# A mixer recorded as tasks with element-exact dependencies and issued from a list schedule

## The chip, the cores and the metric

The kernel runs on one core of one Trainium2 chip. The metric is the device time of one execution in microseconds. TensorE (PE) multiplies matrices, PEld is its weight load, VectorE (DVE), ScalarE (ACT) and GpSimd (POOL) work on tiles in the on-chip memories SBUF and PSUM, and SyncE (SP) mostly issues DMA transfers. Each engine runs its own instructions in the order in which the program lists them and waits on semaphores for the others. So the order on each engine is a part of the program.

## The reference

A decoder trunk of two layers over 16 learned tokens and 1024 input tokens, model width 1024, everything in float32. Layer 0 mixes tokens by RWKV-7 (8 heads of 64) beside a pooling mixer, layer 1 by differential attention; an MLP stands behind each. The part that the change touches is layer 0's mixer:

```python
y = h @ w_in                                   # 1024 -> 14 tiles shifted, 4 pooled
ys = ys + (prev - ys) * mu                     # shift by one token
def step(S, inp):                              # the recurrence, over tokens
    r_t, w_t, k_t, v_t, kk_t, a_t = inp
    sa = jnp.einsum('bhvk,bhk->bhv', S, -kk_t)
    S = (S * w_t[:, :, None, :] + sa[..., None] * (kk_t * a_t)[:, :, None, :]
         + v_t[..., None] * k_t[:, :, None, :])
    o = jnp.einsum('bhvk,bhk->bhv', S, r_t)
    return S, o
o = group_norm(o) * ln_w + ln_b + bonus        # then times a gate g
z = pooled differences of u (windows 2, 4, 8, 16) @ pool_w
return jnp.concatenate([o, z], axis=-1) @ w_out
```

## The kernel before

Activations lie with channels on the 128 partitions and tokens along the free dimension, in blocks of 346 or 348 tokens for the projections and 260 (`NH`) for the output projection. A float32 product is made of three matmuls in a faster format (`mm3`, lines 213 to 219): high part of the weights times high part of the input, low times high, high times low.

Layer 0's mixer is `mixer0` (line 1331). After the entry and `lora` (low-rank paths; their tiles are `psl`, `psg`, `lg`), about 82 us into the run, it works on four things that depend on one another loosely:

- `project` (line 976): one of 18 tiles of the input projection into PSUM tile `ps`, shifted and written to DRAM (`yd`).
- `prep` (line 1094) for each of four head pairs: products within chunks of 64 tokens (tiles `w`, `zb`, `pss`, `sa`, `sb`, `sg`), packed and written to DRAM as `pk`. `invert` (line 1190): 31 small VectorE steps (`tm`, `xi`) that invert the chunks' triangular blocks, read back as `ds`.
- `chain` (line 1216) for each head pair: 17 chunks in groups of up to two, nine groups. Each group loads `lt`, makes block-diagonal tiles `bd` on POOL, three rounds of matmuls into `xs` with copies `x1` (ScalarE) and differences `x2` (VectorE) between them, then `gb`, `qp`, `mk`, `qq`, and for each chunk the output `ob` and the next state: two matmuls accumulate into `sp` (lines 1267 and 1269), and ScalarE writes `S` from it. Every four chunks the output is normed (tiles `ft`, matmul line 1283) and written to DRAM as `ozd`.
- `early` (line 359): parts of the output projection whose inputs exist (PSUM tile `pse`, 18 matmuls each, copied to `pz` by ScalarE and sent to DRAM as `part`), and `pool_group` (line 1292).

What sets the order is a table, `PLAN` (line 60), of stages; `braid` (line 283) takes one step after another from the generators of a stage, at the rates in the table. The instructions are then placed by the framework's scheduler, with program order as their priority. The last two stages read

```python
(('early', 8, 4), ('invert', 3, 3), ('chain', 2, 1)), (('early', 24, 1), ('chain', 3, 2))
```

Behind the mixer stands `late` (line 402): the rest of the output projection, norms and the MLP. It is built otherwise: each piece of work is a task in a `Flow` (line 76), with an engine, a cost by formula and names that it reads and writes; `order` (line 112) ranks each task by the longest path behind it and fills a list schedule; `run` (line 160) issues the tasks in this order, which the framework then keeps. `late_weight` (line 394) loads two of its weights, `wl`, ahead of the last stage through SP's queue; ScalarE rounds each into a high part (`opb`) and VectorE takes the rest.

Of the kernel before, what the change touches and what calls it, by code (L numbers as in the profile page):

```python
# [7 lines left out]
F32 = mybir.dt.float32  # L8
# [67 lines left out]
class Flow:  # L76
# [6 lines left out]
    def add(self, eng, cost, fn, r, w, port=False, size=0, tail=0.0):  # L83
# [8 lines left out]
        i = len(self.tasks)  # L92
        self.tasks.append((eng, cost, fn, deps, port, size, tail))
        for x in r:
            self.read.setdefault(x, set()).add(i)
        for x in w:
            self.wrote[x] = i
            self.read[x] = set()

# [65 lines left out]

class Trunk:
# [18 lines left out]
    def nm(self, s):  # L185
        self.uid += 1
        return f"{s}{self.uid}"

# [24 lines left out]
    def mm3(self, ps, ws, xs, first=True, last=True):  # L213
        nc = self.nc
        n = len(ws)
        for i, ((wh, wl), (xh, xl)) in enumerate(zip(ws, xs)):
            nc.tensor.matmul(ps, wh, xh, start=(first and i == 0), stop=False)  # L217
            nc.tensor.matmul(ps, wl, xh, start=False, stop=False)  # L218
            nc.tensor.matmul(ps, wh, xl, start=False, stop=(last and i == n - 1))  # L219
# [174 lines left out]
    def late_weight(self, l, i, ne):  # L394
        nc = self.nc
        raw = self.R[0][:, i % 2, :self.lw_n[i]]
        hi, lo = self.lw(i)
        nc.sync.dma_start(raw, self.lw_src(l, i))
        nc.scalar.copy(hi, raw)
        nc.vector.tensor_tensor(lo, raw, hi.bitcast(F32), op=ALU.subtract)  # L400

    def late(self, l, xs, part, hin, hmid, hout, pre, rsb):
# [107 lines left out]
        for i in range(len(n)):  # L510
            hi, lo = self.lw(i)
            if l or i > 1:
                z = ("R", i % 4 // 2, i % 2)
                raw = R[i % 4 // 2][:, i % 2, :n[i]]
                F.dma(lambda raw=raw, i=i: nc.sync.dma_start(raw, self.lw_src(l, i)), n[i] * 512, w=[z])
# [506 lines left out]
    def yload(self, mt, a, b):  # L1022
        y = self.yp.tile([P, 320], F32, tag="yl", name=self.nm("yl"), bufs=5)
        self.ylq.dma_start(y[:, :b - a], self.yd[mt, :, a + 1:b + 1])
        return y
# [91 lines left out]
    def prep_group(self, p, g0, m, e, ys, la, bo):  # L1117
# [45 lines left out]
        sb = self.mps.tile([P, 2, 4, C], F32, tag="p", name=self.nm("sb"))  # L1163
        for i in range(m):
            nc.tensor.matmul(sa[:, i, 2:4], kbd[:, i], w4[:, i, 1:3], start=True, stop=True)
        for i in range(m):
            nc.tensor.matmul(sa[:, i, 0:2], bbd[:, i], w4[:, i, 1:3], start=True, stop=True)
        for i in range(m):
# [3 lines left out]
        nc.vector.tensor_tensor(sg[:, :m, 0:4:2], sa[:, :m, 0:4:2],  # L1172
                                cb[:, None, None, B_MA:B_MA + C].broadcast_to([P, m, 2, C]), op=ALU.mult)
        nc.scalar.copy(sg[:, :m, 1:4:2], sa[:, :m, 1:4:2])
# [41 lines left out]
    def chain(self, p):  # L1216
# [5 lines left out]
        for f0, f1 in ((0, 1), (1, 5), (5, 9), (9, 13), (13, 17)):  # L1222
            ob = self.ops_.tile([P, 2, 4 * C], F32, tag="o", name=self.nm("ob"))
            for g0 in range(f0, f1, 2):
# [33 lines left out]
                for i in range(n):  # L1258
# [3 lines left out]
                    if gi:  # L1262
                        nc.tensor.matmul(ob[:, 0, io], S, qq[:, i, 1], start=True, stop=False)
                    nc.tensor.matmul(ob[:, 0, io], vb, qq[:, i, 0], start=gi == 0, stop=True)
                    if gi + 1 < NCH:
                        sp = self.fps.tile([P, P], F32, tag="s", name=self.nm("sp"))
                        nc.tensor.matmul(sp, mk[:, i, 0], vb, start=True, stop=gi == 0)
                        if gi:
                            nc.tensor.matmul(sp, mk[:, i, 1], S, start=False, stop=True)
                        S = cp.tile([P, P], F32, tag="S", name=self.nm("S"), bufs=3)  # L1270
# [8 lines left out]
            bon, gg, sq, x, rs = [ft() for _ in range(5)]  # L1279
# [5 lines left out]
            d = x  # L1285
# [6 lines left out]
    def pool_group(self, gi):  # L1292
# [3 lines left out]
        for t0, W in self.ch:  # L1296
            n = 16 + W
            u = tile()
            nc.sync.dma_start(u[:, :n], self.yd[14 + gi, :, PAD + 1 + t0 - 16:PAD + 1 + t0 + W])
            s = u  # L1300
            step = 1
            while step < win:
                x = tile()
# [4 lines left out]
            if t0 == 0:  # L1308
                ic = cb[:, B_IC + 16 * gi:B_IC + 16 * gi + 16]
                x = tile()  # L1310
# [20 lines left out]
    def mixer0(self):  # L1331
# [10 lines left out]
        with tc.tile_pool(name="yp", bufs=4) as self.yp:  # L1342
# [9 lines left out]
            with tc.tile_pool(name="dps", bufs=4, space=PSUM) as self.dps, \  # L1352
                 tc.tile_pool(name="mps", bufs=4, space=PSUM) as self.mps:
                with tc.tile_pool(name="lyp", bufs=1) as lyp:
# [10 lines left out]
                    self.lora(ly)  # L1365
            self.nw = 2
# [10 lines left out]
            with tc.tile_pool(name="dps", bufs=2, space=PSUM, reuse_waits="tile") as self.dps, \  # L1377
# [5 lines left out]
                 tc.tile_pool(name="cp", bufs=5, reuse_waits="tile") as self.cp:  # L1383
# [10 lines left out]
                with tc.tile_pool(name="pp", bufs=6, reuse_waits="tile") as self.pp:  # L1394
                    self.rwkv_tiles()
                    for _ in proj(*(4, 0, 8)[1:]):
                        pass
                    xs = [[] for _ in self.quarters]
                    rest = self.early(xs, A["wo_0"], part, 6, 6)
                    make = {"prep": self.prep, "invert": self.invert, "chain": self.chain, "proj": lambda a: proj(*a), "pool": lambda a: pools(*a),  # L1400
                            "load": lambda a: self.loads(xs, self.ozd, a, 0, 4), "early": lambda n: itertools.islice(rest, n)}
                    stage = lambda items: self.braid([(make[kind](arg), rate) for kind, arg, rate in items])
                    for items in PLAN[:-1]:
                        stage(items)
                self.base = contextlib.ExitStack()
                pool = self.base.enter_context(tc.tile_pool(name="base", bufs=1, side="right", reuse_waits="tile"))
                self.R = [pool.tile([P, 2, 1024], F32, name="raw0")]
                self.WP = [pool.tile([P, 2, 512], F32R, name=self.nm("wp")) for _ in range(3)]
                self.rsp = contextlib.ExitStack()
                self.rsa = self.rsp.enter_context(tc.tile_pool(name="rsp", bufs=1, side="right", reuse_waits="tile")).tile([P, T], F32, name="rsa")  # L1410
                self.ahead(0)
# [456 lines left out]
```

## Time and profile before

| | us |
|---|---|
| median of three runs | 2830.45 (2830.03 to 2833.7) |
| the profiled execution | 2842.85 |
| its span, first to last instruction | 2841.0 |
| mixer, from the first recorded work to the last chain's norm | 82 to 688, 606 |
| seam from there to the late part's dense start | 688 to 706 |

The profile comes from one execution, which took 12.4 us more than the median. In its rows "out<-in" names the tiles written and read, without their numbers; "x" is a count; a bracket says how long the engine had been idle before the row and which event ended that. A float32 matmul that isn't split runs as two passes and has two records ("x2" in a row of one matmul).

### The profile page before, as it was taken

What the parts mean: (1) busy time and instruction counts of PE and PEld (TensorE: products, weight loads), DVE (VectorE), ACT (ScalarE), POOL (GpSimd) and SP (SyncE); (2) the same over time, 40 slices, a digit from 0 to 9 for tenths busy, and PEclk for the clock granted to TensorE, in tenths of its full rate; (3) what the DMA queues carried; (4) which work ended last, traced back from release to release, by engine and by line L of the source; (5) the groups of instructions that cost most, each with busy time, mean ns of one, the idle gap of its engine ahead of it and who ended that gap; (6) DMA issues with size and microseconds to landing.
All of it is one profiled execution on the core that took longest, in us unless ns stands there. A gap on an engine that the chain in (4) does not pass through costs nothing.

```text
span 2841.0 us, 44543 instructions
## 1 busy us (share of the span) xinstructions
PE 2628.2 (93%) x16822; PEld 2383.3 (84%) x16822; DVE 2098.4 (74%) x3889; ACT 1321.1 (47%) x2719; POOL 306.1 (11%) x404
## 2 busy tenths in 40 slices
PE   7989896888999999999968999999889999999997
PEld 6988786787989999999957888998786788778777
DVE  6558667563787778787795788878638788778888
ACT  5555564533543335433352555565635333344332
POOL 1111224221000000000012222322000000000000
PEclk9999896999999999999988999999999999999998
DMA  4655556554423446433342222222243243544443
GB/s 171 213 166 184 183 174 194 167 172 144 180 83 142 165 154 234 160 128 113 125 133 67 55 70 64 73 70 64 75 145 135 110 159 127 200 171 144 148 156 119
DMA packets 181894, 393.29 MB, mean 138 GB/s; under 512 B 42768, under 2 KB 105616, under 8 KB 169264
## 3 DMA queue, kind: packets, MB, share of 16 engines
q1 hardware_dynamic: 154496, 350.27, 37.2%
q10 hardware_dynamic: 27184, 40.18, 4.0%
q8 instruction: 132, 2.16, 0.3%
q14 instruction: 82, 0.67, 0.1%
HBM read 241.24 MB, written 132.24 MB: 131 GB/s over the span
## 4 chain that ended last, share of the span: by engine, by line
PE 62%; DVE 8%; ACT 2%; issue 2%; DMA 2%; POOL 0%; DVEq 0%; SPq 0%; ACTq 0%
PE bank L537 45%; PE psq L217 2%; PE psq L218 2%; PE psq L219 2%; PE s L1608 1%; PE s L1610 1%; PE tr L1654 1%; DMA hh<-hid 1%; ACT p L1627 1%; DVE opb L664 1%; PE bank L579 1%; PE av L1680 1%; DVE p L1640 1%; DVE ac L919 1%; DVE ac L918 1%
## 5 line engine op out<-in xcount | busy, mean ns | idle before, releaser
L537 PE MATMUL bank<-opa,wp 128*128 128x260 f32 (+1 forms) x3296 | 657.8, 319 | 9.8 <-ACT wp L627 3.7
L537 PEld LDWEIGHTS bank<-opa,wp 128*128 128x128 f32 x3296 | 518.1, 189 | 60.5 <-DVE wp L628 4.7
L537 PE MATMUL bank<-opb,wp 128*128 128x260 f32 (+1 forms) x1150 | 348.5, 324 | 3.0 <-DVE ac L847 3.0
L537 PE MATMUL bank<-opa,hh 128*128 128x260 f32 (+1 forms) x1112 | 240.6, 321 | 7.2 <-DVE hh L628 5.3
L537 PEld LDWEIGHTS bank<-opb,wp 128*128 128x128 f32 x1150 | 216.8, 189 | 22.3 <-ACT opa L870 3.4
L537 PE MATMUL bank<-opa,opb 128*128 128x260 f32 (+4 forms) x1168 | 206.9, 308 | 18.2 <-ACT opa L237 7.0
L847 DVE TENSOR_TENSOR ac<-bank,ac 128x520 f32<-128x520 f32 (+1 forms) x256 | 170.8, 689 | 68.3 <-PE bank L537 65.8
L537 PEld LDWEIGHTS bank<-opa,hh 128*128 128x128 f32 x1112 | 185.7, 191 | 23.7 <-DVE hh L628 5.8
L537 PEld LDWEIGHTS bank<-opa,opb 128*128 128x128 f32 x1168 | 169.5, 195 | 29.2 <-ACT opa L237 7.7
L537 PE MATMUL bank<-opb,hh 128*128 128x260 f32 (+1 forms) x616 | 180.5, 326 | 0.0
L627 ACT CAST wp<-raw 128x512 fp32r<-128x512 f32 (+1 forms) x138 | 80.4, 584 | 199.4 <-PE bank L537 191.9
L627 ACT CAST wp<-ss 128x512 fp32r<-128x512 f32 (+1 forms) x130 | 76.3, 589 | 166.0 <-PE bank L537 143.8
L217 PE MATMUL ps<-opa,whi 128*128 128x346 f32 (+1 forms) x432 | 144.7, 335 | 0.0
L219 PE MATMUL ps<-opa,whi 128*128 128x346 f32 (+1 forms) x432 | 143.0, 331 | 0.5 <-DVE opa L315 0.5
L218 PE MATMUL ps<-opa,wlo 128*128 128x346 f32 (+1 forms) x432 | 143.0, 331 | 0.0
L1627 ACT ACTIVATE p<-s,m 128x272 f32<-128x272 f32 (+7 forms) x128 | 95.5, 750 | 86.7 <-DVE m L1623 84.8
L537 PE MATMUL bank<-opa,tt 128*128 128x260 f32 (+1 forms) x648 | 131.4, 320 | 2.2 <-DVE ac L847 2.0
L537 PEld LDWEIGHTS bank<-opb,hh 128*128 128x128 f32 x616 | 117.3, 190 | 9.9
L217 PE MATMUL psq<-opa,wp 128*128 128x346 f32 (+2 forms) x352 | 118.0, 335 | 4.4 <-DVE rp L302 2.6
L203 POOL TENSOR_TENSOR wpx<-raw,wp 128x1024 fp32r<-128x1024 f32 (+1 forms) x14 | 34.4, 2459 | 794.9 <-PE bank L537 750.6
L219 PE MATMUL psq<-opa,wp 128*128 128x346 f32 (+2 forms) x352 | 113.9, 324 | 0.0
L537 PEld LDWEIGHTS bank<-opa,tt 128*128 128x128 f32 x648 | 102.9, 190 | 11.7 <-issue 2.2
(408 smaller groups left out, 6944.7 us busy)
## 6 DMA issues: line engine op xcount, KB each, us to landing
raw<-in_w_dram SPq DMA_DIRECT2D x64, 1024.0 KB, 4.9
hid<-ac SPq DMA_DIRECT2D x14, 1820.0 KB, 6.1
hid<-ac SPq DMA_DIRECT2D x14, 1792.0 KB, 6.0
hh<-hid SPq DMA_DIRECT2D x23, 1040.0 KB, 7.6
hh<-hid SPq DMA_DIRECT2D x23, 1024.0 KB, 6.8
pk<-sg ACTq DMA_DIRECT2D x32, 704.0 KB, 4.3
lt<-pk SPq DMA_DIRECT2D x32, 704.0 KB, 4.7
raw<-in_w_qkv_dram SPq DMA_DIRECT2D x24, 512.0 KB, 3.6
```

The source lines that it names most:

```text
L203: (lo or nc.gpsimd).tensor_tensor(lw[:, :n], raw[:, :n], hi[:, :n].bitcast(F32), op=ALU.subtract)
L217: nc.tensor.matmul(ps, wh, xh, start=(first and i == 0), stop=False)
L218: nc.tensor.matmul(ps, wl, xh, start=False, stop=False)
L219: nc.tensor.matmul(ps, wh, xl, start=False, stop=(last and i == n - 1))
L537: nc.tensor.matmul(ps, use(x), use(y), start=start and i == j == 0, stop=i == len(ws) - 1 and j == 2, skip_group_check=not start)
L579: nc.tensor.matmul(acc, ones, use(src), start=first, stop=last)
L627: F.act(n, lambda: nc.scalar.copy(use(t[0][:, :n]), src), r=rd, w=[z[0]] + claim)
L664: F.dve(4 * NH, lambda: tt(lo, use(src), hi.bitcast(F32), op=ALU.subtract), r=rd + wh, w=wl)
L847: F.dve(NH, lambda d=d, q=q: tt(sv(d), q, sv(d), op=ALU.add), r=nq + nd, w=nd, ps=True)
L918: F.dve(W, lambda d=d, k=k: stt(d, d, self.gcol(l, 3, k), y, op0=ALU.mult, op1=ALU.mult), r=nd + [ny], w=nd)
L919: F.dve(W, lambda d=d, k=k: tt(d, d, use(H3[k // 4][:, k % 4, :W]), op=ALU.add), r=nd + [("H", k // 4, k % 4)], w=nd)
L1627: nc.scalar.activation(p[:, :L0], S[c][:, :L0], AF.Exp, bias=m2[:, c:c + 1], scale=0.125, accum_out=m2[:, 2 + c:3 + c])
```

## The change

Everything in `mixer0` after `lora` runs with a `Recorder` in place of the engine handle. It keeps each call as a task. `region` turns an operand into sets of elements, one for each dimension of its tensor, and `keep` makes a task depend on the earlier ones whose elements it shares, where one of the two writes. At the end `Flow.order` makes the list schedule and the calls are issued in that order. `group` holds calls together as one task: the three matmuls of `mm3`, the pair into `ob`, the pair into `sp`.

Pools give fixed tiles, in turn, from a `Ring`: so tiles of one ring all carry the name of its first user (`pse` and `pst` become `ps`, `sb` becomes `sa`, `qp` becomes `xs`, `ho` and `pz` become `yt`, `x1` becomes `x`). `S` has two tiles in place of three; a norm uses four `ft` tiles in place of five; `sb` is taken after `sa` was copied out; `pool_group` alternates two tiles. The pools for the late part are opened after the mixer's are closed. `late_weight` is gone: its loads, roundings and differences are tasks of `late`, in both layers, and the loads are issued by POOL. Every engine runs the same number of instructions of each operation as before, but that four DMAs moved from SP to POOL.

```diff
-        i = len(self.tasks)
-        self.tasks.append((eng, cost, fn, deps, port, size, tail))
+        i = self.push(eng, cost, fn, deps, port, size, tail)
...
+class Ring:
+    def tile(self, shape, dtype, tag=None, name=None, bufs=None):
...
+        ring = self.rings[tag]
+        ring[0] += 1
+        t = ring[1][(ring[0] - 1) % n][:, :free]
...
+class Recorder:
+    def group(self):
+        self.held = []
+        yield
+        calls, self.held = self.held, None
...
+    def call(self, eng, op, args, kw):
...
+        if op.startswith("dma"):
+            cost, size = .06, 4 * math.prod(int(k) for k in out.shape)
+        elif eng == "PE":
+            cols, x = math.prod(int(k) for k in args[0].shape[1:]), args[1]
+            if x.dtype == F32R:
+                cost = max(cols / 2400 + .014, .108)
+            elif x.dtype == F32:
+                cost = 2 * max(2 * cols / 2400 + .003, .111)
...
+        elif eng == "DVE":
+            cost = n / 960 + .07 + (.06 if psum else 0.0)
+        elif eng == "ACT":
+            cost = n / 1200 + .1 + (.1 if hasattr(kw.get("scale"), "ap") else 0.0)
+        else:
+            cost = n / 450 + .15
...
+    def keep(self, eng, cost, fns, r, w, port, size):
+        deps = set()
+        r, w = [[(x.tensor.name, self.region(x)) for x in y] for y in (r, w)]
+        hit = lambda a, b: all(x & y for x, y in zip(a, b))
+        for name, m in r:
+            deps.update(i for i, a, wr in self.seen.get(name, ()) if wr and hit(a, m))
+        for name, m in w:
+            deps.update(i for i, a, wr in self.seen.get(name, ()) if hit(a, m))
+        i = self.flow.push(eng, cost, lambda: [f() for f in fns], deps, port, size)
...
-    def late_weight(self, l, i, ne):
...
-            if l or i > 1:
+            if True:
...
-                F.dma(lambda raw=raw, i=i: nc.sync.dma_start(raw, self.lw_src(l, i)), n[i] * 512, w=[z])
+                q = "POOL" if i < 2 else "SP"
+                F.dma(lambda raw=raw, i=i, q=q: (nc.gpsimd if q == "POOL" else nc.sync).dma_start(raw, self.lw_src(l, i)), n[i] * 512, w=[z], eng=q)
...
-                        S = cp.tile([P, P], F32, tag="S", name=self.nm("S"), bufs=3)
+                        S = cp.tile([P, P], F32, tag="S", name=self.nm("S"), bufs=2)
...
-            bon, gg, sq, x, rs = [ft() for _ in range(5)]
+            bon, gg, sq, rs = [ft() for _ in range(4)]
...
+            rec = Recorder(tc)
+            self.nc = nc = rec
+            entered = self.wp, self.yp
+            self.wp, self.yp = Ring(self.wp, 2), Ring(self.yp, 4)
...
+                for x, n in (("dps", 2), ("mps", 1), ("nps", 1), ("chp", 2), ("ops_", 1), ("fps", 1), ("cp", 4), ("pp", 6)):
+                    setattr(self, x, Ring(getattr(self, x), n, 0 if x in ("cp", "pp") else 512))
...
-                    for items in PLAN[:-1]:
-                        stage(items)
...
-                self.ahead(0)
-                for i in (0, 1):
-                    self.late_weight(0, i, 6)
-                stage(PLAN[-1])
+                for items in PLAN:
+                    stage(items)
...
+                rec.flow.run()
+            self.nc = tc.nc
+            self.wp, self.yp = entered
```

ScalarE during the third chain, before: rows between one `S` and the next; `pz` are the copies of finished early parts, `part` their DMAs, `opa` high parts of early inputs.

```order
L1271 ACTIVATE S_6081<-sp_6078,pcs 128x128
L237 CAST opa_73<-ho_5746 128x260
L1249 COPY gb_755<-xs_6115 64x4x64
...
L367 COPY pz_5783<-pse_5764 128x260
L368 DMA part_89<-pz_5783 128x260
L237 CAST opa_77<-ho_5754 128x260
L367 COPY pz_5805<-pse_5786 128x260
...
L367 COPY pz_5992<-pse_5973 128x260
L368 DMA part_89<-pz_5992 128x260
L367 COPY pz_6014<-pse_5995 128x260
L1271 ACTIVATE S_6142<-sp_6139,pcs 128x128
```

In all, eight `pz` copies stand between the two `S` rows. ScalarE near the end of that chain in the changed kernel, where `yt` are the copies of early parts out of the ring tiles `ps`:

```order
L267 ACTIVATE S_1_811<-sp_0_809,pcs 128x128
L267 CAST opa_75<-yt_1_765 128x260
L267 CAST opa_77<-yt_0_764 128x260
L267 COPY gb_753<-xs_0_801 64x4x64 x2
L267 COPY yt_1_765<-ps_1_763 128x260
L267 ACTIVATE S_0_810<-sp_0_809,pcs 128x128
L267 COPY yt_0_764<-ps_0_762 128x260
L267 DMA part_89<-yt_1_765 128x260
L267 DMA part_89<-yt_0_764 128x260
L267 COPY x_1_804<-xs_0_801 128x256
L267 ACTIVATE S_1_811<-sp_0_809,pcs 128x128
```

One or two copies stand between two `S` rows there. POOL at the end of the third chain in the changed kernel, with the load of `wl` that stood on SP:

```order
L267 TENSOR_TENSOR ft415_2_814<-ft415_2_814,ft415_1_813 128x256
L267 TENSOR_TENSOR bd407_0_799<-ds260_0_793,conb_98 128x2x128
L267 TENSOR_TENSOR bd407_0_799<-lt406_2_798,conb_98 128x2x128
L643 DMA raw0_6209<-in_wl_0_dram 128x768 x2
L267 TENSOR_TENSOR bd407_1_800<-lt406_0_796,conb_98 128x128
L267 TENSOR_TENSOR bd407_1_800<-ds260_1_794,conb_98 128x128
```

The two loads stand between the `bd` products of two chain groups. TensorE at the end of the last chain and the start of the late part, before (`bank` are the late part's PSUM tiles):

```order
L1264 MATMUL ob1236_6933<-qq1259_7028,lt1253_7003 128x64
L218 MATMUL pse1293_7289<-opa7_77,wlo1286_7220 128x260
L219 MATMUL pse1293_7289<-opa7_77,whi1285_7219 128x260
L1283 MATMUL ob1236_6933<-ft1264_7041,conb_98 128x256
L537 MATMUL bank0_7372<-opa1_71,opb1124_6482 128x260 x3
L537 MATMUL bank0_7372<-opa1_71,opb1125_6483 128x260 x3
```

And the same place in the changed kernel:

```order
L267 MATMUL ob405_0_795<-qq412_1_808,lt406_2_798 128x64
L267 MATMUL ob405_0_795<-ft415_2_814,conb_98 128x256
L665 MATMUL bank3_6246<-opa0_70,opb1273_6229 128x260 x12
L665 MATMUL bank3_6246<-opa1_71,opb1273_6229 128x260 x12
L665 MATMUL bank0_6243<-opa1_71,opb1271_6220 128x260 x3
L665 MATMUL bank0_6243<-opa1_71,opb1272_6221 128x260 x3
```

The first late matmuls used `opb1124`, a part of `wl`; now they use `opb1273`, a part of `wo`, whose raw load SP issues behind the loads of `ho`.

160 lines of the change are left out of this document (121 added, 39 removed).

## The prediction

> **What bounds the kernel now.** I read the page first, for who is busy and what ends the span; then the table of stretches, to see where the engines stand idle; then the timeline of TensorE inside two stretches, to see what a matmul costs there; and the table of stretches again for single tiles.
>
> The page (busy share in 40 slices of 71 us, the granted clock in tenths, and the shares of the chain that ended last):
> ```profile
> span 2841.0 us, 44543 instructions
> PE   7989896888999999999968999999889999999997
> PEclk9999896999999999999988999999999999999998
> PE 62%; DVE 8%; ACT 2%; issue 2%; DMA 2%; POOL 0%; DVEq 0%; SPq 0%; ACTq 0%
> ```
> TensorE ends nearly everything. Its weak slices, the ones at 8, 6 and 8 from the fifth to the tenth, lie in the first layer's mixer, which the change touches. The mixer's stretches, cut where its four chains begin (each chain is a recurrence over 17 chunks, worked in 9 groups), then the seam to the late part, and the start of that part (columns: bounds, length, then busy us and count for PE, PEld, DVE, ACT, POOL; granted clock; DMA share; GB/s):
> ```profile
> 82.00:280.00 198.00, 182.22 (x1216) 176.18 (x1215) 134.30 (x397) 103.56 (x335) 33.13 (x84) 0.97 0.55 176
> 280.00:400.00 120.00, 104.49 (x712) 95.80 (x711) 88.11 (x264) 70.16 (x232) 31.68 (x53) 0.93 0.62 196
> 400.00:537.00 137.00, 106.75 (x654) 98.09 (x653) 90.51 (x268) 75.30 (x250) 51.94 (x68) 0.82 0.60 185
> 537.00:626.00 89.00, 76.62 (x549) 70.68 (x549) 50.47 (x125) 31.52 (x86) 20.17 (x24) 0.92 0.47 142
> 626.00:688.00 62.00, 60.41 (x468) 55.57 (x467) 23.73 (x57) 26.19 (x75) 16.19 (x22) 1.00 0.47 142
> 688.00:706.00 18.00, 8.41 (x39) 7.11 (x39) 6.25 (x13) 5.88 (x14) 0.72 (x1) 0.72 0.48 151
> 706.00:781.00 75.00, 72.31 (x542) 70.09 (x543) 54.18 (x92) 40.36 (x70) 0.00 (x0) 0.98 0.52 192
> ```
> I call the first five A to E, 606 us together. PE's busy time counts each matmul to its end, though the next starts sooner, so it overstates the work. The timeline gives the true pace (start, length, line, names):
> ```profile
> 86.35 0.32 PE L217 MATMUL ps<-opa,whi 128*128 128x346 f32 x1
> 86.51 0.32 PE L218 MATMUL ps<-opa,wlo 128*128 128x346 f32 x1
> 555.30 0.28 PE L218 MATMUL pse<-opa,wlo 128*128 128x260 f32 x1
> 555.42 0.28 PE L219 MATMUL pse<-opa,whi 128*128 128x260 f32 x1
> 552.98 0.39 PE L1252 MATMUL qp<-lt,gb 128*128 128x128 f32 x2
> 553.21 0.39 PE L1253 MATMUL qp<-lt,gb 128*128 128x128 f32 x2
> ```
> A projection matmul (ps) costs 0.16 us, an early matmul of the output projection (pse) 0.12, a small one of chain and preparation 0.22 for its two records, 0.11 each. How many of the first two stand in a stretch, the same table says for their tiles alone (pse in C, D, E; ps in A, B, C; columns as above, PE and PEld, for ps DVE and ACT too, for pse ACT):
> ```profile
> 400.00:537.00 137.00, 5.46 (x24) 3.73 (x24) 0.00 (x0) 0.82 0.60 185
> 537.00:626.00 89.00, 39.79 (x252) 33.57 (x252) 5.62 (x15) 0.92 0.47 142
> 626.00:688.00 62.00, 27.26 (x156) 20.93 (x156) 3.01 (x9) 1.00 0.47 142
> ...
> 82.00:280.00 198.00, 144.78 (x814) 129.99 (x814) 16.97 (x33) 0.00 (x0) 0.97 0.55 176
> 280.00:400.00 120.00, 43.14 (x189) 31.67 (x188) 4.11 (x8) 3.28 (x6) 0.93 0.62 196
> 400.00:537.00 137.00, 22.18 (x99) 16.12 (x98) 2.05 (x4) 3.28 (x6) 0.82 0.60 185
> ```
> So TensorE's work is: A 814 x 0.16 + 402 x 0.11 = 174 us; B 189 x 0.16 + 523 x 0.11 = 88; C 99 x 0.16 + 24 x 0.12 + 531 x 0.11 = 77; D 252 x 0.12 + 297 x 0.11 = 63; E 156 x 0.12 + 312 x 0.11 = 53. Set beside the largest engine of each stretch, **how full the stretch is**: A 174/198 = 0.88 (PE), B 88/120 = 0.73 (PE and DVE alike), C 90.5/137 = 0.66 (DVE), D 63/89 = 0.71 (PE), E 53/62 = 0.85 (PE). The late part, which a list schedule orders already, has 542 x 0.12/75 = 0.87. In A and E, TensorE is the bound. In B, C and D nothing is: 346 us in which the engines wait for each other in turn.
>
> One such turn, in D (TensorE twice, then VectorE, whose bracket says how long it had stood idle and for what):
> ```profile
> 556.65 0.44 PE L1267 MATMUL sp<-lt,mk 128*128 128x128 f32 x2
> 568.64 0.38 PE L1269 MATMUL sp<-S,mk 128*128 128x128 f32 x2
> 568.68 0.19 DVE L1208 TENSOR_TENSOR tm<-li,xi 68x31 f32<-68x31 f32 x1 [10.81 <-DMA li<-ldd]
> ```
> Two halves of one state update stand 12 us apart. S, the second half's operand, needs one ScalarE instruction; but ScalarE's order puts eight copies of pse results ahead of it, each behind 18 early matmuls on TensorE (the first block of order rows above). The chain stood still for filler that could have gone anywhere. That is a fault of order.
>
> **The change, part by part.** Nearly every instruction of the mixer stays, with its form; so the sum is over stretches: new work of the largest engine, divided by how full it gets.
>
> *Where work goes.* Counted in the built order between chain starts, 46 ps matmuls move into A, half each out of B and C; early matmuls become 6 in C, 102 in D, 324 in E. PE work is then A 174 + 46 x 0.16 = 181.4; B 84; C 71; D 63 - 150 x 0.12 = 45; E 53 + 168 x 0.12 = 73. VectorE's instructions, counted so and priced by the rows of their shapes, move little: B 88.1 to 84.6, C 90.5 to 87, D 50.5 to 53.5.
>
> *A and E*, bound by TensorE, I leave as full as they are: A 181.4/0.88 = 206 (+8), E 73/0.88 = 83 (+21; 0.88 and not 0.85, since added filler stands in the chain's gaps).
>
> *B, C and D.* The new order mixes by longest path and interleaves the copies with the chain's S (second order block: two copies between S and S, not eight). Bounds for how full these get: 0.73, what B reaches now, and 0.95, a little under E's clean rows (60.4 busy of 62, 0.97). I take 0.83, nearest the late part's 0.87, and below it because each chain group is a row of short steps on four engines: B 84.6/0.83 = 102 (-18), C 87/0.83 = 105 (-32), D 53.5/0.83 = 64.5 (-24.5).
>
> *The start.* The last ScalarE copy of the part before, lg, stood here:
> ```profile
> 83.89 0.43 ACT L1069 COPY lg<-psg 128x346 f32<-128x346 f32 x1
> ```
> TensorE fills with projection matmuls around it. In the new order its first recorded matmul (pss) waits for a ScalarE square that stands behind all of these copies, and a projection's weights stand behind writes on SP's queue. From 82 to 84.3 is 2.3 us, plus a short step: +3, bounds 0 and 6.
>
> *The seam.* TensorE's late matmuls before the dense stretch, and the SP load whose weight is the first operand in the new order:
> ```profile
> 690.66 1.08 PE L537 MATMUL bank<-opa,opb 128*128 128x260 f32 x3 [1.82 <-ACT opa L237]
> 696.89 6.24 PE L537 MATMUL bank<-opa,opb 128*128 128x260 f32 x33 [5.14 <-ACT opa L237]
> 700.35 0.35 SPq L515 DMA_DIRECT2D raw<-in_wo_dram  x1
> 706.56 0.63 PE L537 MATMUL bank<-opa,opb 128*128 128x260 f32 x3 [0.87 <-DVE opb L517]
> ```
> In the new order the first late matmuls need the weight that is loaded last, 6 us before 706.56; the 37 that ran ahead (37 x 0.12 = 4.4 us) come behind it. +5, bounds 0 and +8.
>
> *The two wl loads* go from SP's queue to POOL's. On SP they were issued early and cost its queue this:
> ```profile
> 619.24 1.62 SPq L398 DMA_DIRECT2D raw<-in_wl_dram  x2
> raw<-in_wo_dram SPq DMA_DIRECT2D x11, 384.0 KB, 3.5
> ```
> Behind them on SP stood three of the last chain's lt loads, now 1.6 us freer. On POOL they stand among the last chain's bd products (third block), with later bd behind them and TensorE's xs behind those. No row shows a load of a kernel tensor from POOL. From the nearest row, 3.5 us to landing, ScalarE's cast of wl could stand 0 to 4 us in front of the chain's S. I take 0, the cast being a group later, and keep 4. In the second layer the load has this room:
> ```profile
> 2071.68 0.33 SPq L515 DMA_DIRECT2D raw<-in_wl_dram  x1
> 2081.63 1.67 ACT L516 CAST opb<-raw 128x640 fp32r<-128x640 f32 x2 [0.40 <-ACT pz L367]
> ```
> Ten us lie between load and cast, whose own wait is for pz: 0, bounds -2 and +2. The Trainium skill speaks against this move: "DMA: Bandwidth & Descriptors", section "SWDGE vs HWDGE vs iDMA", says that transfers issued from GpSimd are built by software and written to rings in SBUF that VectorE can lock GpSimd out of. By its fit (2.0 us and bytes over 436e3 per us) 393 KB would take an estimated 2.9 us, no more than the row's 3.5; no run here shows the lock-out, and the sum stays as it is.
>
> *Buffers.* S has two tiles instead of three, ft four instead of five, and sb is taken after sa is emptied. Longest of the waits around S:
> ```profile
> ACT S L1271 <- PE sp L1269: 60.1, 45, 4.4
> PE sa L1167 <- ACT zb L1188: 25.2, 10, 11.0
> ```
> S waits for sp, its producer, and not for a free tile; a new S can only be made after the one before is used. 0; the other end is the second rival. The last row, 25 us of sa waiting for the preparation's zb in ten pieces, is the sort of wait that an order can remove.
>
> *Sum:* A +8, start +3, B -18, C -32, D -24.5, E +21, seam +5 = -37.5. On the profiled execution's 2842.85 us (span 2841.0 and 1.85 around it) that is 2805; the median shown is 2830.45, 12.4 lower, so **2793 us**.
>
> The clock is a term apart. Granted clock is 0.82 in C and 0.72 in the seam, where TensorE idles most, against 0.97 and more in A and E. In C it is about 77/0.82 - 77 = 17 us of TensorE's time, included in "how full". The Trainium skill, "TensorE: Matmul & The Clock Gate", Part 1, says that the array falls to half rate after an idle window of some 3.4 us and comes back after as long a busy one; the clock column agrees in direction. By that rule pauses cut short would be worth up to those 17 us once more, an estimate inside the next rival.
>
> **The rivals.**
>
> *Tight packing.* The order fits so well that all five stretches reach 0.95: (181.4 + 84.6 + 87 + 53.5 + 73)/0.95 = 505 + 3, so -98, and the seam +5: -93, **2737**. For it: nothing but order holds B to D. Against it: the late part, ordered the same way, has 0.87.
>
> *As full as before.* The work is shifted, but each stretch stays as full as it was: A 206 + 3, B 84.6/0.73 = 116, C 87/0.66 = 132, D 53.5/0.71 = 75, E 73/0.85 = 86: 618, +12, and the seam +5: +17, **2847**. This is also the case in which the change does not do what it says. For it: the list knows costs by formulas, and in-order engines pay for each that is wrong. Against it: the 12 us turn above goes for certain.
>
> *Latency of the chain, slower than before.* A chain group is a row of steps xs, x1, xs, x2, xs, gb, qp, mk, sp, S, each on another engine, over rings of fixed tiles (S two, qp and xs sharing two PSUM tiles). If these rings and not the order set the groups' pace, B, C and D keep 346 us, while A, E and the seam still pay: 8 + 3 + 21 + 5 = +37, **2867**. It decides from a group pace of (346 - 37)/27 = 11.4 us on, over 27 groups; the forecast has 271.5/27 = 10.1, before 12.8. Against it: E runs 9 groups in 62 us, 6.9 each, over the same tiles.
>
> **How the numbers follow.** Forecast 0.55, its own range 2770 to 2815; tight packing 0.17; as full as before 0.15; latency 0.13. The range 2740 to 2850 leaves out half of the tight case (0.08) and nearly all of the latency case (0.12). About 0.2%, 5.7 us, is what a measurement can tell from no change. Faster by more: 0.52 of the forecast, 0.17, and 0.02 of the third = 0.71. Within: 0.03 + 0.04 + 0.01 = 0.08. Slower: 0.09 + 0.12 = 0.21.
>
> **What would show it.** The recorded instructions will carry one line, so the tiles tell: the first xs of each chain should stand near 291, 393, 498 and 562 us, and the last ob near 645. Right: no two halves of an sp over 2 us apart, PE's clock in the second and third stretch over 0.9. Wrong: bd or S waits that grow at POOL's wl load; TensorE idle at the start by more than 6 us; chain groups at 11.4 us or more; a seam over 26 us. A change after 800 us would be one that I have not priced.

## The result and the profile after

The changed kernel takes 2902.36 us (median of four runs, 2901.44 to 2905.17), the kernel before 2832.07 us beside it: a ratio of 1.0247, with a 95% interval from 1.0229 to 1.0265. It is 70 us slower, where 37 us less was forecast.

The page of the changed kernel: span, TensorE's busy share and granted clock in 40 slices, and the shares of the chain that ended last.

```profile
span 2899.7 us, 44524 instructions
PE   7896686769799999999987899999899999999997
PEclk9998898879899999999998899999999999999998
PE 64%; DVE 9%; issue 3%; ACT 3%; DMA 2%; POOL 0%; ACTq 0%; DVEq 0%; SPq 0%; POOLq 0%
```

The loss lies in the first eleven slices, in the mixer and the seam; from the twelfth on, the row of TensorE reads like the one of before, a slice later. The table of stretches of the changed kernel, cut at the first `xs` of each chain, which belongs to a group of one chunk (bounds, length, then busy us and count for PE, PEld, DVE, ACT, POOL; granted clock; DMA share; GB/s):

```profile
82.00:317.00 235.00, 195.15 (x1259) 187.77 (x1260) 142.56 (x402) 112.40 (x348) 36.82 (x93) 0.93 0.50 160
317.00:442.00 125.00, 94.70 (x688) 87.77 (x686) 86.51 (x258) 71.13 (x229) 36.87 (x55) 0.92 0.56 173
442.00:576.00 134.00, 93.31 (x606) 85.55 (x605) 86.21 (x260) 72.59 (x233) 43.37 (x61) 0.85 0.59 180
576.00:669.00 93.00, 59.66 (x402) 54.47 (x402) 52.38 (x136) 29.83 (x85) 21.56 (x28) 0.82 0.46 131
669.00:748.50 79.50, 76.82 (x644) 75.64 (x643) 22.85 (x58) 33.24 (x89) 19.44 (x23) 1.00 0.47 143
748.50:765.00 16.50, 1.17 (x4) 0.47 (x3) 5.53 (x12) 5.32 (x11) 0.72 (x1) 0.54 0.45 151
```

By the same rule the third chain before starts at 527 us (its first `xs` stands at 526.94) and not at 537, where the table before the change was cut. So its C was 127 us and its D 99; the 346 us of B, C and D together stand.

```profile
400.00:527.00 127.00, 98.28 (x600) 90.26 (x599) 85.05 (x253) 70.70 (x235) 50.07 (x65) 0.81 0.59 181
527.00:626.00 99.00, 85.10 (x603) 78.50 (x603) 55.94 (x140) 36.12 (x101) 22.03 (x27) 0.91 0.49 152
```

| stretch | before | forecast | after |
|---|---|---|---|
| A | 198 | 209 | 235 |
| B | 120 | 102 | 125 |
| C | 127 | 105 | 134 |
| D | 99 | 64.5 | 93 |
| E | 62 | 83 | 79.5 |

The work went where the forecast put it: TensorE's busy time rises by 13 and 16 us in A and E and falls by 10, 5 and 25 in B, C and D. But B, C and D, which should have become 74.5 us shorter together, became 6 longer. TensorE is busy for 0.76, 0.70 and 0.64 of them, where it was 0.87, 0.77 and 0.86. The chains start at 317, 442, 576 and 669 us, where 291, 393, 498 and 562 were forecast.

Mixer and seam account for 59 us, the difference between the two profiled executions. That of the kernel before had taken some 11 us more than the median; most of that stands behind the mixer, as part 5 of the experiments shows.

One place in A shows why. The timeline, first of SP's queue, then of VectorE, then of TensorE (start, length, line, names; the bracket is the idle time before the row and what ended it):

```profile
215.19 15.74 SPq L267 DMA_DIRECT2D li<-ldd  x4
231.03 4.98 SPq L267 DMA_DIRECT2D raw<-in_w_in_dram  x1
237.43 0.19 DVE L267 TENSOR_TENSOR tm<-li,xi 68x31 f32<-68x31 f32 x1 [18.51 <-DMA li<-ldd]
241.35 0.65 PE L267 MATMUL ps<-opa,whi 128*128 128x346 f32 x1 [18.84 <-DVE ys L267]
```

The four `li` loads that feed an inversion hold SP's queue for 15.7 us. VectorE's next row is the first step of that inversion. It stands 18.5 us in front of all of VectorE's later work, also of the `ys` step that would empty a PSUM tile for TensorE. So three engines stop for these loads. It happens once for each inversion: the table of waits (for what, us in total, times, longest) of the changed kernel has

```profile
DVE tm L267 <- DMA li<-ldd: 76.0, 4, 21.1
```

and that of the kernel before, where the same step came to stand behind other causes as well,

```profile
DVE tm L1208 <- DMA li<-ldd: 20.6, 2, 10.8
DVE tm L1208 <- DMA yl<-yd: 13.1, 1, 13.1
DVE tm L1208 <- issue: 9.7, 1, 9.7
```

TensorE's pauses at these four places are 18.8, 19.8, 16.5 and 15.9 us, 71 together. Before, they were 11.0, 6.3 and 10.2 us at the first three, 27.5 together. At the fourth, TensorE ran early matmuls through VectorE's whole wait; its next pause, 4.6 us long, was ended by ScalarE's `S` (the rows stand with the account of the prediction below). The first of them, 11.0 us, shows the other way in which these loads stop TensorE: its operand `zb` waited for a `yl` load, which SP issued behind them (kernel before; SP, ScalarE, TensorE).

```profile
183.07 22.15 SPq L1200 DMA_DIRECT2D li<-ldd  x4
205.32 4.98 SPq L1024 DMA_DIRECT2D yl<-yd  x1
212.14 0.30 ACT L1187 COPY zb<-yl 64x128 f32<-64x128 f32 x1 [12.81 <-DMA yl<-yd]
215.54 0.80 PE L1167 MATMUL sa<-w,zb 128*128 128x128 f32 x2 [11.04 <-ACT zb L1188]
```

### The profile page after: what moved, and what is told of

It is laid out like the page before. It is cut to its first block, busy times and chain, and to the rows that moved or that the text cites. A ratio compares the mean times of both kernels' runs of the same rounds, so it can differ in the third digit from the quotient of the medians.

```text
span 2899.7 us, 44524 instructions
## 1 busy us (share of the span) xinstructions
PE 2616.9 (90%) x16822; PEld 2375.9 (82%) x16822; DVE 2101.0 (72%) x3889; ACT 1333.5 (46%) x2719; POOL 310.1 (11%) x408
## 4 chain that ended last, share of the span: by engine, by line
PE 64%; DVE 9%; issue 3%; ACT 3%; DMA 2%; POOL 0%; ACTq 0%; DVEq 0%; SPq 0%; POOLq 0%
PE bank L665 45%; PE psq L352 2%; PE psq L353 2%; PE psq L354 2%; PE ps L267 2%; PE s L1746 1%; PE tr L1792 1%; PE s L1748 1%; PE xs L267 1%; ACT p L1765 1%; PE bank L707 1%; DMA yt<-ozd 1%; PE av L1818 1%; PE sp L267 1%; DVE p L1778 1%
## 5 line engine op out<-in xcount | busy, mean ns | idle before, releaser
L267 PE MATMUL ps<-opa,whi 128*128 128x346 f32 (+2 forms) x1008 | 273.0, 332 | 54.8 <-DVE ys L267 45.4
L267 PEld LDWEIGHTS ps<-opa,whi 128*128 128x128 f32 x1008 | 183.2, 195 | 56.5 <-DVE ys L267 46.0
L665 PEld LDWEIGHTS bank<-opa,opb 128*128 128x128 f32 x1168 | 168.8, 195 | 33.5 <-ACT opb L644 18.5
L267 PE MATMUL ps<-opa,wlo 128*128 128x346 f32 (+2 forms) x504 | 159.6, 317 | 0.0
L665 PE MATMUL bank<-opb,opb 128*128 128x256 f32 (+4 forms) x456 | 111.4, 308 | 1.4 <-DVE tt L721 1.4
```

The source lines that it names most:

```text
L267: one = eng, cost, lambda: fn(*args, **kw), r, w
L665: nc.tensor.matmul(ps, use(x), use(y), start=start and i == j == 0, stop=i == len(ws) - 1 and j == 2, skip_group_check=not start)
```

## Experiments

**1. Is it the list's belief about the load?** The recorder costs a DMA at 0.06 us of its queue and 2 us of landing plus its bytes over 350e3 per us. The first theory (A) is that this belief puts the inversion step too early; its rival (B), from the prediction, is that rings of tiles set the pace.

```diff
         if op.startswith("dma"):
             cost, size = .06, 4 * math.prod(int(k) for k in out.shape)
+            if out.tensor.name.startswith("li"):
+                cost, size = 3.9, 1.47e6
```

> The changed kernel, where only the recorder's cost of the four li loads of an inversion is altered: 3.9 us of SP's queue and 4.2 us of bandwidth each (about 23 us from the first issue to the last landing, as the trace has it: 215.19 to 237.43), in place of 0.06 us and 0.2 us of bandwidth each. Theory A (the list schedule believes the li loads land at once, so VectorE's order puts the first inversion step right behind them, and VectorE with all its later work waits 17.8 to 21.1 us, four times): the four pauses of TensorE (18.8, 19.8, 16.5 and 15.9 us, 71 together) fall to under 35 together, and the time to 2850 to 2875 us. Theory B (fixed rings of tiles, two S and shared PSUM tiles, set the chain's pace): the pauses move but the time stays within 10 us of 2902.

Measured: 2884.25 us, 18 less, between both theories. VectorE's waits before the four first steps shrank from 76 to 17 us, but TensorE's pauses less: three of 9.6, 14.1 and 25.6 us are left, 49 in place of 71. The timeline of this run at the last one, SP and then TensorE:

```profile
541.35 16.85 SPq L269 DMA_DIRECT2D li<-ldd  x3
558.30 5.46 SPq L269 DMA_DIRECT2D yt<-ozd  x2
563.86 1.98 SPq L269 DMA_DIRECT2D ds<-xd  x4
568.32 0.80 PE L269 MATMUL xs<-lt,bd 128*128 128x128 f32 x2 [25.57 <-POOL bd L269]
```

The next inversion's loads now hold up the `ds` loads, the results of the inversion before, which the next chain needs. So the load is not only late, it also stops what is queued behind it.

**2. Order or buffers?** The same recorder, rings and tiles, but the calls are issued as recorded and the framework places them.

```diff
-                rec.flow.run()
+                for t in rec.flow.tasks:
+                    t[2]()
```

> The changed kernel with the same recorder, rings, buffers and wl loads, but the recorded calls are issued in the order in which they were recorded and the framework's scheduler places them, as in the kernel before; the list schedule of the mixer is left out. Theory A (the loss comes from the list's order): near the kernel before, 2825 to 2850 us. Theory B (the loss comes from rings, two S tiles, four ft tiles): 2880 us or more.

2857.35 us, 7 past theory A's band and far under theory B's: 45 of the 70 us come with the list's order, as long as the loads are slow. The other 26, against the kernel before beside it (2831.19), are in what the run shares with the change. Of it, the `wl` loads on POOL were tried alone (`q = "SP"` for all of them):

> The changed kernel with the two wl loads of each layer issued by SP again, behind the wo load. Theory A and theory B alike: the mixer's four chains stand where they were within 3 us, the time within 6 us of 2902. A third theory (the loads on POOL hold up bd products, and so the last chains): the last two chains get at least 6 us shorter together.

2900.67 us, as both theories had it: the third theory falls. The queue of these loads costs nothing here.

**3. The load itself.** Over the middle of the first pause, the table of stretches of the changed kernel reads

```profile
222.00:236.00 14.00, 0.51 (x5) 0.31 (x3) 0.00 (x0) 0.98 (x3) 0.00 (x0) 0.70 0.09 14
```

A DMA share of 0.09 is 1.4 of 16 engines, and 14 GB/s. An `li` load has 17 partitions, one for each chunk. The Trainium skill, "DMA: Bandwidth & Descriptors", section "Why a DMA increments its semaphore by 16 and not by 1", says that a transfer is spread over the largest number of engines up to 16 that divides the slowest dimension of both its patterns; 17 is prime, and that leaves one. The share of 1.4 engines, with some other transfers in it, is near that. So each load was issued as two, of 16 partitions and of 1:

```diff
         for hs in range(4):
-            self.invq.dma_start(li[hs * NCH:(hs + 1) * NCH], ld[..., :, ...])
+            for c0, c1 in ((0, 16), (16, NCH)):
+                self.invq.dma_start(li[hs * NCH + c0:hs * NCH + c1], ld[..., c0:c1, ...])
```

in the changed kernel and in the kernel before:

> The changed kernel, where each of the four li loads of an inversion (17 partitions, 68 KB) is issued as two, of 16 partitions and of 1. In the trace of the changed kernel the DMA engines are 0.09 to 0.13 busy in the four pauses, at 14 to 24 GB/s, so a 17-partition load seems to run on about one of 16 engines. Theory A (the pauses are VectorE's wait for slow li loads): SP spends under 6 us, not 15.7, on an inversion's li loads, the four pauses (71 us) fall to under 30, the time from 2902 to 2840 to 2865 us. Theory B (rings and buffers set the pace): the pauses go, but their work only moves, and the time stays above 2885.

> The kernel before with the same split of the li loads and nothing else. It has four pauses at the same loads (11.0, 6.3, 10.2 and 4.6 us, 32 together), and VectorE stands idle 43 us there. Theory A: the pauses go and the time falls by 20 to 40 us, to 2792 to 2812. If the loads' length doesn't come from the 17 partitions: no change, 2825 to 2837.

The changed kernel falls by 61 us to 2841.03, as theory A had it. The timeline of that run at the place shown first, SP and VectorE:

```profile
215.88 5.36 SPq L267 DMA_DIRECT2D li<-ldd  x8
222.99 0.19 DVE L267 TENSOR_TENSOR tm<-li,xi 68x31 f32<-68x31 f32 x1 [3.40 <-DMA li<-ldd]
```

The first step stands 7 us behind the first issue and not 22, and in the table of waits the four first steps wait 15.7 us together and not 76.0. Its stretches:

```profile
82.00:307.00 225.00, 197.95 (x1260) 188.88 (x1259) 144.17 (x403) 112.71 (x349) 37.21 (x93) 0.95 0.53 169
307.00:413.00 106.00, 95.09 (x686) 88.09 (x685) 87.01 (x263) 70.46 (x229) 37.26 (x54) 0.98 0.64 198
413.00:530.00 117.00, 90.21 (x605) 81.21 (x605) 84.32 (x257) 73.28 (x234) 46.35 (x62) 0.94 0.67 211
530.00:606.00 76.00, 61.34 (x401) 56.26 (x402) 51.39 (x132) 29.03 (x83) 22.28 (x29) 0.85 0.55 157
606.00:685.00 79.00, 76.63 (x643) 75.45 (x642) 22.91 (x59) 32.99 (x89) 19.44 (x23) 1.00 0.47 142
```

With the slow load out of the way, B, C and D are 299 us, 47 less than before: the list does fill them better. A, at 225, and E, at 79, take it back.

The kernel before wins only 5 us by the same edit (2824.58, ratio 0.9981, interval 0.9971 to 0.9990), where 20 to 40 were expected: a miss. Its stretches are A, then B to D, then E:

```profile
82.00:273.00 191.00, 181.91 (x1212) 176.09 (x1211) 134.45 (x396) 101.08 (x328) 33.72 (x83) 0.98 0.57 181
273.00:615.50 342.50, 287.61 (x1935) 264.86 (x1936) 233.40 (x653) 177.67 (x570) 109.38 (x147) 0.90 0.58 180
615.50:681.00 65.50, 59.62 (x444) 54.32 (x444) 25.25 (x63) 28.61 (x80) 14.07 (x20) 0.97 0.47 148
```

TensorE's idle time in the mixer goes from 75.5 us to 70 only (606 less 530.5 busy, 599 less 529.1), though the long pauses at the loads are gone: other, shorter waits took their place. The likely reason is that the old order covered the loads. It issues the next preparation's groups (one or two `ldd` writes between the last one that an inversion needs and its first step, at three of the four) and early matmuls while they run, and its first inversion step stands at 211.7 us with slow loads and with split ones, though SP had issued the first split ones by 190.4; the third stands at 433 and 432 us. In the changed order no `ldd` write stands there: the change took this cover away. That the cover is the whole difference between 5 and 61 us was not tested.

**4. Is the priority wrong?** In A no preparation group starts between 107 and 161 us, while projections run. A further theory (C) is that the longest path, counted through reuse of tiles, makes projections look urgent. Two ways to alter that: the plan's order as the priority (`rank = [-float(i) for i in range(len(T))]` in the mixer's list), and, with the split loads, the longest path along true dependencies alone.

> The changed kernel, where the mixer's list schedule takes, among the tasks that can start, the one recorded first (the plan's order) and not the one with the longest path behind it; costs, rings and loads as in the change. Theory C (the longest path is misled by tile reuse: projections pile up at 117 to 157 us while VectorE and ScalarE idle and no preparation group starts): first chain starts before 300 us (317 in the change, 280 before), time 2860 to 2880. Theory A alone (only the cost of the li loads misleads it): within 12 us of 2902.

> Both edits together: the split li loads and, in the mixer's list, the plan's order as priority. Theory A (the four pauses of 72 us in the run with plan priority are li loads): 2909 less 55 to 65, 2843 to 2855. Theory C (the plan's order also removes the pile of projections before the first chain): the first chain stays before 285 us and the gain adds, to 2815 to 2835.

> As the run with split li loads and the seam restored, but the longest path is counted along true dependencies (a read of what another wrote) and not through reuse of tiles; waits and buffers stay. Theory C (reuse of tiles makes projections look urgent, so preparation stands still from 107 to 161 us): the first chain starts before 285 us instead of 307, the time falls to 2800 to 2830. Without C: 2833 to 2845, or slower.

2909.32, 2854.61 and 2865.86 us. The first chain does start early (276, 264 and 233 us), and the time is no better than with the list as it was: 7 us worse unsplit, 14 worse with split loads, and 33 worse than the run with the seam restored, below. In the last run the chains end at 670 us and TensorE's dense late work starts at 720: 340 early matmuls had been left to the end, so this run says little of the rank alone. None of the three bears theory C out; starting the first chain early was worth nothing by itself. The two runs with plan priority differ by 55 us, and the split alone sets them apart: theory A again.

**5. The seam.** In the change the first late matmuls need `wo`. SP's row of its load, then TensorE's:

```profile
758.78 0.33 SPq L643 DMA_DIRECT2D raw<-in_wo_dram  x1
763.56 0.59 PE L665 MATMUL bank<-opa,opb 128*128 128x260 f32 x1 [14.60 <-ACT opb L644]
764.88 1.45 PE L665 MATMUL bank<-opa,opb 128*128 128x260 f32 x5 [0.73 <-DVE opb L645]
```

Next the split loads with layer 0's two `wl` weights out of the late part's list again, still on POOL's queue; the loads, roundings and differences stand ahead of it:

```diff
-            if True:
+            if l or i > 1:
...
         self.ahead(0)
+        for i in (0, 1):
+            self.late_weight(0, i, 6)
```

> The changed kernel with split li loads, and layer 0's two wl weights again outside the late part's task list (loaded, rounded and subtracted ahead of it, on POOL's queue), so that its first matmuls need wl and not wo. If the seam term holds (37 matmuls run ahead of wo, 3 to 5 us): 2841 falls to 2835 to 2839, and the first bank matmul stands within 6 us of the last ob. If it falls to under 2832, the seam cost more than I worked out.

2833.29 us, 7.7 less. TensorE's late matmuls in that run:

```profile
688.22 1.21 PE L673 MATMUL bank<-opa,opb 128*128 128x260 f32 x3
694.54 6.98 PE L673 MATMUL bank<-opa,opb 128*128 128x260 f32 x33 [5.12 <-ACT opa L267]
704.80 1.45 PE L673 MATMUL bank<-opa,opb 128*128 128x260 f32 x5 [0.93 <-DVE opb L653]
```

The 37 matmuls run ahead of `wo` again, at 688 to 702 us. The term of the prediction holds in kind, and was +5 against 7.7. The ends of the profiles say the same: behind the last chain, the kernel before with split loads takes 2143 us (681 to 2824.0) and the changed kernel 2151 (748.5 to 2899.7), 8 more. The profiled execution of the kernel before took 2153 there (688 to 2841.0), though it runs the same code behind the mixer; so some 10 of its extra 11 us lie there, and the table of stretches didn't show the seam.

**6. What is left of the buffers.** Recorded order, split loads and the seam restored, against the kernel before with split loads:

> Recorder, rings and fewer S and ft tiles as in the change, split li loads, the seam restored, and the recorded order given to the framework's scheduler. Against the kernel before with split li loads (2824.6) only rings, buffers, the grouped matmuls and POOL's queue for wl differ. Theory B (they cost time): 2835 to 2850. If they cost nothing: 2820 to 2830.

> The run with split li loads and the seam restored (2833.3), with three S tiles as in the kernel before instead of two. If the second S tile was costed rightly at nothing: 2830 to 2837, chain groups unchanged. Theory B (S's ring holds up the chains): under 2827.

The first took 2837.31 us, 13 more than the kernel before with split loads, as theory B had it; so rings, fewer tiles, grouped matmuls and `wl` on POOL come with about that under the framework's scheduler. By the profiles 7 of it lie in the mixer (82 to 688 against 82 to 681) and 5 behind it. Which of them costs it was not tried. It is also only 4 us from the list's order with the same loads and seam (2833.29): the list's order costs 45 us with the slow loads and nothing that shows with the split ones. It is the two together that lost the time. The second, the run of part 5 with a third S tile, took 2842.91, 10 more, a miss for both theories. A third tile takes waits away and adds none; but it alters the list, and another list can be 10 us worse. So a difference of 10 us between two orders, the 13 above too, shows little of its reason.

**7. Honest costs for every DMA.** With the split loads and the seam restored, the recorder's DMAs cost 0.35 us of their queue, as the rows have it, and 3.5 us to land, in the mixer alone; then 3.0 and 4.0 us, for the scatter just seen.

```diff
-            cost, size = .06, 4 * math.prod(int(k) for k in out.shape)
+            cost, size = .35, 4 * math.prod(int(k) for k in out.shape)
...
+                rec.flow.land = 3.5
                 rec.flow.run()
```

> The run with split li loads and the seam restored (2833.3), where the recorder's DMA costs follow the trace: 0.35 us of the issuing queue (rows show 0.32 to 0.35) in place of 0.06, and 3.5 us to land in place of 2.0, in the mixer alone. Theory A in general form (what the list loses is what its costs don't know of DMAs): 2815 to 2828, below the kernel before. If the li loads were the only DMA that mattered: 2830 to 2837.

> The run with DMA costs of 0.35 us and 3.5 us (2814.4), with 3.0 us to land. If the gain comes from honest costs: 2810 to 2825. If it was luck of one list: anywhere from 2815 to 2845.

> The same with 4.0 us to land. If the gain comes from honest costs: 2810 to 2825. If it was luck of one list: anywhere from 2815 to 2845.

2814.44, 2825.28 and 2819.28 us, against 2833.29 with the first costs. All three are better, by 8 to 19 us; the middle one is a little past the band that was set. Three gains of three point to the costs; they don't say how much of the best one is luck of its list, nor which of the two costs did it. The 2814.44 beats both kernels: its ratio to the kernel before is 0.9949 (0.9936 to 0.9963). Against the kernel before with the same split loads (2824.58) the three are 10 us faster, 1 us slower and 5 us faster, no more than the scatter seen in part 6. The last run has these costs, the `li` cost of part 1 and the loads unsplit:

> Honest DMA costs in the mixer's list (0.35 us to issue, 3.5 us to land, li loads 3.9 us of SP and 4.2 us of bandwidth each), the seam restored, but the li loads unsplit as in the change. If the order alone lost the time: within 10 us of the 2814.4 of the run with split loads. If the slow loads hold SP's queue whatever the order: 2840 to 2870, the first-chain ds or yl loads again behind them.

2877.99 us, 8 past the band for loads that hold the queue. With the honest costs, the `li` ones too, the slow loads still take back 64 us. SP, VectorE and TensorE at the fourth inversion of that run:

```profile
557.88 15.59 SPq L270 DMA_DIRECT2D li<-ldd  x4
579.12 0.87 SPq L270 DMA_DIRECT2D lt<-pk  x2
579.96 0.19 DVE L270 TENSOR_TENSOR tm<-li,xi 68x31 f32<-68x31 f32 x1 [11.39 <-DMA li<-ldd]
583.67 1.19 PE L270 MATMUL xs<-lt,bd 128*128 128x128 f32 x4 [13.12 <-DMA lt<-pk]
```

The chain's own `lt` loads stand behind the inversion's loads, and TensorE waits 13.1 us for them.

## Why the prediction was wrong, step by step

**B, C and D (-74.5 forecast, +6 measured) is the step that failed: the fullness of 0.83, with no price for the `li` loads.** I took the idle time of these stretches for a fault of order that the list would mend. By VectorE's busy time, from which the forecast divided, they became 0.69, 0.64 and 0.56 full. The loads hold SP's queue for 15 to 17 us at each inversion, VectorE waits 76 us for them and TensorE stands still for 71. Once they were split, the same list filled the stretches to 0.82, 0.72 and 0.68, and B, C and D gave 47 of the 74.5 us. VectorE's rows for all four inversions were there before. So were 21 of the 25 us of `sa` waiting for `zb`, which I called the sort of wait that an order can remove: its pieces of 11.0 and 10.2 us are the pauses at the first and third inversion.

My example, the turn in D, was read wrongly. I put the 12 us between two halves of a state update down to the eight copies in ScalarE's order. ScalarE's two `S`, TensorE's early matmuls alone in that turn (`pse`; busy time and count of PE, PEld, ACT), and TensorE's next pause:

```profile
551.20 0.37 ACT L1271 ACTIVATE S<-sp,pcs 128x128 f32<-128x128 f32 x1 [1.25 <-PE sp L1269]
557.70:568.60 10.90, 10.87 (x90) 10.87 (x90) 1.51 (x4) 1.00 0.24 64
574.46 0.37 ACT L1271 ACTIVATE S<-sp,pcs 128x128 f32<-128x128 f32 x1
574.88 0.69 PE L1263 MATMUL ob<-qq,S 128*128 128x64 f32 x2 [4.64 <-ACT S L1271]
```

The S that the second half reads was written at 551.20, before the first half. Between the halves TensorE ran 90 early matmuls without a gap, because its own order has them there; the turn cost it no time, and nothing was sure to be won there. The copies stand ahead of the next S and held TensorE up for 4.6 us. The third row of the fence in the prediction had the wait to price: VectorE idle for 10.81 us until an `li` load. The old order ran matmuls meanwhile. In the changed kernel TensorE stood still for 15.9 us at that inversion.

**A (+8) and the start (+3)**, measured +37. About 8 of it is the pause at the first `li` load (18.8 against 11.0 us). The start is larger than its bound of 6: ScalarE's rounding of a projection's weights, behind their load, then TensorE:

```profile
94.81 1.04 ACT L267 CAST whi<-raw 128x1024 fp32r<-128x1024 f32 x1 [3.70 <-DMA raw<-in_w_in_dram]
97.73 0.66 PE L267 MATMUL ps<-opa,whi 128*128 128x346 f32 x1 [6.74 <-DVE ys L267]
```

The mechanism was near the one named: the weights came late, and the `ys` step that empties a tile for TensorE stood behind VectorE's part of their rounding. The size is 6.7 us in this one pause. The moved projections brought about their 8. The rest of A, some 14 us, is not settled. Theory C was to explain it and didn't. With split loads in both kernels A is still 34 us longer (225 against 191): TensorE is busy 16 us longer there, and idle 18 us longer. This is a second term that was too small, and it stays when the loads are mended: -43.5 in B to D, +34 in A, +13.5 in E and the seam leave a span of 2836.0 us against 2824.0, and no gain.

**E (+21)** was 17.5 in the change and 17 with the loads split; the work did move there, as counted in the order. **The seam (+5)** was right in kind, and 7.7 by the run that undid it. **The wl loads and S at nothing:** right for the queue of the loads (-1.7 us measured); for S there is no sign that two tiles cost time. **The clock** was to be over 0.9 in B and C: it was 0.92 and 0.85, and 0.98 and 0.94 with the loads split.

**The rivals.** The latency rival came nearest (2867, slower) and names a wrong mechanism: chain groups did keep their pace (352 us over 27 groups, 13.0 each), but not because of rings; the same rings run at 11.1 once the loads are split (299 over 27). None of the rivals priced a load that stops its queue.

## What to carry to other kernels

An idle row that a DMA ends is a price to be carried into the new order. What stood beside it may have been its cover: here the order that had it lost 5 us by the slow loads, and the one without it 61. A list schedule of in-order engines depends on its costs for DMAs: here four loads that took seven times as long as the list had them (22 us, where it had 4 x 0.06 + 4 x 0.2 + 2.0 = 3.0) stopped three engines. Knowing the true cost was not enough either, since the loads also held the queue for all that stood behind them. Before reordering around a slow load, look at how it is spread over the DMA engines: here 16 + 1 partitions in place of 17 was worth 61 us of the changed kernel, and 5 of the kernel before. And before a wait is called a fault of order, look whether the engine that matters was idle in it, and which write its operand came from.

## What the runs showed of the hardware

A load of 17 partitions and 68 KB (544 rows of 128 B) held SP's queue for about 4 us (four in 15.74); while such loads ran, all transfers together moved at 14 GB/s, with 0.09 of the 16 DMA engines busy. The same data as 16 and 1 partitions took under 0.7 us of the queue for each piece on average (eight in 5.36 us), and all eight had landed 7 us after the first issue. A load of 384 KB from POOL's queue landed 7.2 us after its issue in the first layer and 3.8 us (320 KB) in the second; on SP loads of 384 KB took 3.5 us. The 2.9 us that the prediction worked out as an estimate from the fit of the Trainium skill, "DMA: Bandwidth & Descriptors", section "Anatomy of one DMA — SWDGE (gpsimd) path", is not what the first of these shows.
